# A decoder layer on one core: eight small parameter loads asked for behind the 25th load of raw tiles

## The chip, the core and the metric

The kernel runs on one core of a Trainium2 chip. A core has five engines that run side by side and meet at semaphores: TensorE (PE in the profile, with its weight loads as PEld), VectorE (DVE), ScalarE (ACT), GpSimd (POOL) and SyncE (SP). Here SP does no arithmetic: it issues every transfer, one after the other, and sixteen DMA engines carry them out. The metric is device microseconds of one execution. Three runs of the kernel before took 2458.3, 2456.9 and 2456.46 us, a median of 2456.9 us.

## The reference

One layer of a decoder trunk, batch 1, 2048 rows of 1024 values, all in float32:

```
proj = x @ w_in                     # 1024 -> q, k, v (8 heads x 64), b, c, h (256 each), p (256)
attn = stick_breaking_attention(q, k, v)         # sigmoid gates, products over the later keys, causal
conv = b * causal_conv3(c * h, conv_w)
pool = (window means of p over 2, 4, 8, 16, minus p) @ pool_w * pool_scale
mix  = rms_norm per 64 columns of [attn, conv, pool], times mix_norm_g
x1   = layer_norm(2**0.25 * x + mix @ w_o) * ln1_g + ln1_b
out  = layer_norm(2**0.25 * x1 + relu(x1 @ w_up)**2 @ w_down) * ln2_g + ln2_b
```

The small parameters of the change are `conv_w`, `pool_w` (four 64x64 blocks), `pool_scale`, `mix_norm_g` and `rcount`, a table of one over the number of rows in a window for the first 16 rows.

## The kernel before

Every large product is made of three: each float32 operand is split into a high part (rounded to the matmul's format by ACT) and a low part (the rest, by DVE or POOL), and PE adds high x high, high x low and low x high. `load` does this for the operands of the projections: SP issues the DMA of a raw tile of 128x512 values (L180), ACT casts it (L182), DVE or POOL subtracts (L184). The raw tiles, of x and of the weights alike, go through a ring of `RAW = 4` buffers, so the load of a tile waits on SP until the tile four loads back has been subtracted.

The 2048 rows are four chunks of 512. `qkv(cs)` projects two chunks: for a head group first k (`proj_qk` with `kscr`), then q, then v (`proj_v`). A projection of one chunk and 256 columns is two PSUM banks (`dn`, two buffers) of 24 matmuls each. A bank is emptied by `split`: a cast on ACT (L65, for q with a scale L68) and a subtraction on DVE (L66, L69) into `qk`, which SP writes to DRAM in four pieces per bank (L271, L272). Attention reads k, q and v back from there (L425, L409, L410, L427) and goes through units of 128 queries by 512 keys: a score matmul (`z`, L433), two sigmoids on ACT, a scan on DVE (L443, L446), a product on POOL (L448), transposes (`tp`, L465) and the product with v (`o`, L470, L471). After attention's chunks come `bchp` (conv and pool projections), the output projection and the first norm (`out_stage`), then the up and the down product.

The order of the work is not the order of the code. A scheduler places the instructions of all stages into one queue per engine before the kernel is built, by its own estimate of when each can start and by priorities: `early()` is the highest (loads, casts, subtractions, emptying of banks), attention is next, the projections are last, so PE fills attention's pauses with projections. Each engine then takes its queue strictly in order: an instruction that must wait holds up all that stand behind it. A change anywhere may give the scheduler other estimates, and other queues, for all that follows.

The eight loads of the change stand in the code ahead of everything that uses x: `gain` (L149), `cw` (L151), `psc` (L153), `rcount` (L155) and two pieces each of `pw0` and `pw1` (L160, L161). `gain` is read when a mixer's output is normalised (L302), `cw` in `conv` (L332 to L334), `rcount` and `pw` in the pool mixer (L358, L370), `psc` behind it (L372).

Of the kernel before, what the change touches and what calls it, by code (L numbers as in the profile page):

```python
# [17 lines left out]
P = 128  # L18
# [6 lines left out]
HD = 64  # L25
# [18 lines left out]
def build(nc, tc, ctx, A, out):  # L44
# [78 lines left out]
    with ExitStack() as up:  # L123
        pools = phase1(nc, tc, ctx, up, A, ident, scr, hscr, split, rsqrt, layer_norm, bcast)
# [3 lines left out]
def phase1(nc, tc, whole, ctx, A, ident, scr, hscr, split, rsqrt, layer_norm, bcast):  # L128
# [17 lines left out]
    nc.gpsimd.affine_select(last[:, CH + OFF - P - 1:], last[:, CH + OFF - P - 1:], pattern=[[-1, P + 1]],  # L146
                            compare_op=ALU.not_equal, fill=1.0, base=0, channel_multiplier=1)
    gain = p.tile([P, ND], F, name="gain")
    nc.sync.dma_start(gain, A["mix_g"])  # L149
    cw = pd.tile([P, 2, 3], F, name="cw")  # L150
    nc.sync.dma_start(cw, A["conv_w"])  # L151
    psc = pd.tile([P, 2], F, name="psc")
    nc.sync.dma_start(psc, A["pool_scale"])  # L153
    rcount = pd.tile([P, 2, 16], F, name="rcount")
    nc.sync.dma_start(rcount, A["rcount"])  # L155
    pw = []
    for i in range(2):
        w = pd.tile([P, P], F, name=f"pw{i}")
        nc.vector.memset(w, 0.0)
        nc.sync.dma_start(w[0:HD, 0:HD], A["pool_w"][2 * i])  # L160
        nc.sync.dma_start(w[HD:P, HD:P], A["pool_w"][2 * i + 1])  # L161
        pw.append(w)
    ucar = pd.tile([P, 2, 2], F, name="ucar")
    nc.vector.memset(ucar, 0.0)
# [3 lines left out]
    def early():  # L168
        return tc.high_priority(2 * PRIO)

    count = [0]

    def low_engine():
        count[0] += 1
        return nc.vector if (count[0] % 3 == 0) == (count[0] >= START) else nc.gpsimd

    def load(src, name, shape, bufs):
        pool = px if name == "x" else pm
        raw = pd.tile(shape, F, name=f"{name}raw", tag="raw", bufs=RAW)
        nc.sync.dma_start(raw, src)  # L180
        h = pool.tile(shape, R, name=f"{name}h", tag=f"{name}h", bufs=bufs)
        nc.scalar.copy(h, raw)  # L182
        l = pool.tile(shape, R, name=f"{name}l", tag=f"{name}l", bufs=bufs)
        low_engine().tensor_tensor(l, raw, h.bitcast(F), ALU.subtract)  # L184
        return h, l

    def load_w(g, x=None):

        w, xt = [], []
        with early():  # L190
            for q in range(4):
                w.append(load(A["w_in"][g][q], "w", [P, 2, 256], ND))
                if x is not None:
                    xt += [load_x(x, d) for d in (2 * q, 2 * q + 1)]
        return w, xt

    def load_x(c, d):
        return load(A["xt"][c][d], "x", [P, CH], 2 * ND)
# [42 lines left out]
    def proj_v(xs, g):  # L241
        for c, w, x in operands(xs, 4 + g):
            for jj in range(2):
                ps = dense_ps().rearrange("p (j e) -> p j e", j=2)
                for j in range(2):
                    ts = slice((2 * jj + j) * P, (2 * jj + j + 1) * P)
                    for d in range(ND):
                        wh, wl = (t[:, d % 2, :] for t in w[d // 2])
                        xh, xl = (t[:, ts] for t in x[d])
                        nc.tensor.matmul(ps[:, j, :], xh, wh, start=(d == 0), stop=False)  # L250
                        nc.tensor.matmul(ps[:, j, :], xh, wl, start=False, stop=False)
                        nc.tensor.matmul(ps[:, j, :], xl, wh, start=False, stop=(d == ND - 1))
                with early():
                    vst = pd.tile([P, 2, 4, P], R, name="vst", tag="big", bufs=3)
                    pv = ps.rearrange("p j (h x) -> p j h x", h=4)
                    split(vst[:, :, :, 0:HD], vst[:, :, :, HD:P], pv)
                    for j in range(2):
                        nc.sync.dma_start(vscr[c][g][:, :, 2 * jj + j, :].rearrange("h p x -> p h x"),
                                          vst.bitcast(F)[:, j])
                tick()  # L260

    def proj_qk(xs, g, scr, scale):
        for c, e, ps in proj_t(xs, g):
            with early():
                hl = pd.tile([P, 2, CH], R, name="qk", tag="big", bufs=3)
                hi, lo = hl[:, 0], hl[:, 1]
                split(hi, lo, ps, scale)
                for hh in range(2):
                    t = scr[c][4 * (g % 2) + 2 * e + hh]
                    rows = slice(hh * HD, (hh + 1) * HD)  # L270
                    nc.sync.dma_start(t[0], hi.bitcast(F)[rows])  # L271
                    nc.sync.dma_start(t[1], lo.bitcast(F)[rows])  # L272

    def qkv(cs):
        xs = [(c, []) for c in cs]
        for g in range(2):
            proj_qk(xs, 2 + g, kscr, None)
            proj_qk(xs, g, qscr, 0.125)
            proj_v(xs, g)
# [104 lines left out]
    def attention(c, pairs):  # L384
        for i in pairs:
            mix = {}
            for hh in range(2):
                head(c, 2 * i + hh, mix)

    def run(end=False):  # L390

        while units:
            units.pop(0)()
            turn[0] += 1
            if turn[0] > 5:
                blocks.pop(0)()
        while end and blocks:
            blocks.pop(0)()
            turn[0] = 0
        while end and soon:  # L400
            soon.pop(0)[1]()
# [89 lines left out]
    def load_wo(part):  # L491
        with early():
            w = [[load(A["w_o"][e][:, dd * CH:(dd + 1) * CH], "x", [P, CH], 2 * ND) for e in part] for dd in range(2)]
        wo.extend(zip(*w))
# [75 lines left out]

    turn_out = Turn(nc, tc, pd, ident, tscr, bank, {"b0": "pb", "b1": "pc", "c0": "pa", "x1h": "cs", "x1l": "cs"}, 4, early)

    for cs in ((0, 1), (2, 3)):
        qkv(cs)
        with tc.high_priority(PRIO):
            for pairs in ((0, 1), (2, 3)):
                for c in cs:
                    attention(c, pairs)
            run(True)
# [388 lines left out]
```

## Time and profile before

| | us |
|---|---|
| median of three runs | 2456.9 |
| the profiled execution | 2459.65 |
| its span (first to last instruction) | 2457.9 |
| PE busy in it | 2398.0 |
| DVE busy | 1589.8 |
| POOL busy | 1136.3 |
| ACT busy | 1008.2 |

The span is that of the engines' instructions; the profiled execution's own time is 1.75 us longer. "Busy" of PE is the time in which a matmul is under way; matmuls overlap, so two that stand side by side in a list start closer together than their durations say. A row of the timeline gives a start, a busy time, engine, line, operation and tiles, how many instructions are merged in it, and in brackets the idle time ahead of it with the instruction that ended it.

### The profile page before, as it was taken

To read this page: it belongs to the slowest core of one execution; us is meant where nothing else is said; L and a number is where in the kernel's file an instruction comes from. 1 tells how busy PE (TensorE), PEld (TensorE's weight loads), DVE (VectorE), ACT (ScalarE), POOL (GpSimd) and SP (SyncE) were. 2 spreads that over 40 slices of the span, in tenths; PEclk is the share of its full clock that TensorE was granted. 3 is DMA by queue.
4 is the path that set the end of the run, shared out by engine and by line. 5 is a ranking of instruction groups with operands and counts; after the bars stand their busy time and mean duration, and the time that the engine had idled before them with its cause. 6 is when DMAs were issued, how large, how long until landed. Compare 5 with 4: busy or idle time off the path is not lost.

```text
span 2457.9 us, 33072 instructions
## 1 busy us (share of the span) xinstructions
PE 2398.0 (98%) x11728; PEld 1992.8 (81%) x11728; DVE 1589.8 (65%) x2227; ACT 1008.2 (41%) x1945; POOL 1136.3 (46%) x833
## 2 busy tenths in 40 slices
PE   8999999999999999999999999999999999999997
PEld 6988888778778787788888888888888888888886
DVE  3778777788987899976666656556316433333367
ACT  4667666655666656522333223222332101111123
POOL 2557555864775757634556545555201101101137
PEclk9999999999999999999999999999999999999999
DMA  8758645622422446557665383333525312212212
GB/s 239 193 148 235 174 138 148 195 78 91 158 82 95 141 149 220 201 216 289 221 225 192 112 333 125 116 103 112 173 75 172 110 53 86 86 49 78 80 60 112
DMA packets 164854, 360.37 MB, mean 147 GB/s; under 512 B 18640, under 2 KB 35024, under 8 KB 162896
## 3 DMA queue, kind: packets, MB, share of 16 engines
q1 hardware_dynamic: 164688, 358.25, 45.2%
q8 instruction: 93, 1.52, 0.3%
q14 instruction: 73, 0.60, 0.1%
HBM read 245.19 MB, written 112.98 MB: 146 GB/s over the span
## 4 chain that ended last, share of the span: by engine, by line
PE 78%; DVE 9%; DMA 4%; POOL 4%; issue 3%; ACT 2%; SPq 1%; DVEq 0%; ACTq 0%; POOLq 0%
PE dn L895 9%; PE dn L894 9%; PE dn L893 9%; PE b L792 7%; PE c L792 4%; PE a L792 4%; PE z L433 4%; PE dn L235 3%; PE dn L236 3%; PE b L795 3%; PE dn L237 3%; PE tp L465 3%; PE c L795 2%; PE a L795 2%; PE dn L521 2%
## 5 line engine op out<-in xcount | busy, mean ns | idle before, releaser
L448 POOL TENSOR_TENSOR g<-g,sig 128x512 f32<-128x512 f32 (+2 forms) x320 | 381.6, 1197 | 338.3 <-DVE g L446 144.4
L893 PE MATMUL dn<-d,ht 128*128 128x512 f32 x1024 | 398.3, 389 | 0.0
L894 PE MATMUL dn<-d,ht 128*128 128x512 f32 x1024 | 398.3, 389 | 0.0
L895 PE MATMUL dn<-d,ht 128*128 128x512 f32 x1024 | 397.7, 389 | 0.0
L732 POOL TENSOR_TENSOR w<-raw,w 128x512 fp32r<-128x512 f32 x186 | 253.9, 1371 | 240.9 <-ACT w L731 240.9
L899 DVE TENSOR_TENSOR y<-dn,y 128x512 f32<-128x512 f32 x224 | 154.2, 689 | 322.2 <-PE dn L895 322.1
L858 POOL TENSOR_TENSOR d<-draw,d 128x1024 fp32r<-128x1024 f32 x32 | 77.6, 2438 | 507.4 <-ACT d L857 507.2
L446 DVE TENSOR_TENSOR_SCAN g<-beta,g,z 128x513 f32<-128x513 f32 x192 | 244.1, 1275 | 48.5 <-ACT sig L438 46.3
L436 ACT ACTIVATE beta<-z 128x512 f32<-128x512 f32 (+2 forms) x320 | 172.9, 541 | 159.4 <-PE z L433 146.3
L871 ACT CAST ht<-draw 128x512 fp32r<-128x512 f32 x128 | 74.5, 620 | 380.3 <-PE dn L895 347.3
L895 PEld LDWEIGHTS dn<-d,ht 128*128 128x128 f32 x1024 | 192.2, 188 | 39.9
L893 PEld LDWEIGHTS dn<-d,ht 128*128 128x128 f32 x1024 | 192.2, 188 | 39.9
L894 PEld LDWEIGHTS dn<-d,ht 128*128 128x128 f32 x1024 | 192.2, 188 | 39.9
L731 ACT CAST w<-raw 128x512 fp32r<-128x512 f32 x186 | 114.1, 621 | 252.9 <-PE b L795 143.8
L235 PE MATMUL dn<-xh,wh 128*128 128x512 f32 x512 | 206.9, 407 | 10.3 <-DVE qk L66 5.3
L433 PE MATMUL z<-k,q 128*128 128x512 f32 (+3 forms) x640 | 192.6, 380 | 17.8 <-DVE g L446 12.7
L236 PE MATMUL dn<-xl,wh 128*128 128x512 f32 x512 | 206.8, 404 | 0.0
L237 PE MATMUL dn<-xh,wl 128*128 128x512 f32 x512 | 206.7, 404 | 0.0
L469 DVE TENSOR_TENSOR tl<-tp,th 128x512 fp32r<-128x512 f32 (+1 forms) x320 | 184.3, 596 | 30.3 <-ACT th L468 29.5
L465 PE MATMUL tp<-ident,g 128*128 128x128 f32 x1088 | 190.8, 274 | 1.9 <-DVE tl L469 0.8
L792 PE MATMUL b<-x,w 128*128 128x512 f32 x768 | 190.2, 390 | 2.1 <-ACT w L731 1.5
L468 ACT CAST th<-tp 128x512 fp32r<-128x512 f32 (+1 forms) x320 | 161.5, 535 | 63.9 <-PE tp L465 51.9
(195 smaller groups left out, 4983.9 us busy)
## 6 DMA issues: line engine op xcount, KB each, us to landing
hscr<-h SPq DMA_DIRECT2D x128, 256.0 KB, 2.8
draw<-hscr SPq DMA_DIRECT2D x64, 512.0 KB, 3.9
raw<-in_w_up SPq DMA_DIRECT2D x62, 512.0 KB, 4.4
x<-tscr SPq DMA_DIRECT2D x14, 2048.0 KB, 12.3
wraw<-in_w_in SPq DMA_DIRECT2D x80, 256.0 KB, 3.3
k<-kscr SPq DMA_DIRECT2D x80, 256.0 KB, 3.0
v<-vscr SPq DMA_DIRECT2D x80, 256.0 KB, 2.8
xraw<-in_xt SPq DMA_DIRECT2D x64, 256.0 KB, 3.1
```

What stands on the lines that cost most here:

```text
L235: nc.tensor.matmul(ps, wh, xh, start=(d == 0), stop=False)
L236: nc.tensor.matmul(ps, wh, xl, start=False, stop=False)
L237: nc.tensor.matmul(ps, wl, xh, start=False, stop=(d == ND - 1))
L433: nc.tensor.matmul(z[:, 0:w], q[:, b, j * P:(j + 1) * P], m["k"][:, 0:w], start=(b == 0), stop=(b == 1))
L446: nc.vector.tensor_tensor_scan(left, rev, idle, st["prev"][j][:, OFF - 1:OFF], ALU.mult, ALU.bypass)
L448: nc.gpsimd.tensor_tensor(gv, gv, sig[:, 0:w], ALU.mult)
L465: nc.tensor.transpose(out=tp[:, j * P:(j + 1) * P], in_=m["g"][j][:, cols], identity=ident)
L732: self.nc.gpsimd.tensor_tensor(w[:, 1], src, w.bitcast(F)[:, 0], ALU.subtract)
L792: nc.tensor.matmul(ps, wk[:, 0, d], x[:, i, :, d, :], start=(first and d == 0 and i == 0), stop=False, skip_group_check=True)
L893: nc.tensor.matmul(ps, hh[:, ts], dh[:, ds], start=(i == 0), stop=False)
L894: nc.tensor.matmul(ps, hh[:, ts], dl[:, ds], start=False, stop=False)
L895: nc.tensor.matmul(ps, hl[:, ts], dh[:, ds], start=False, stop=(i == 3))
```

## The change

The eight loads leave the head of the program. A function `parameters` issues them once, after the first `qkv`, and holds each of them behind the 25th raw tile's load: twelve loads belong to the first chunk (four weight tiles, eight of x), eight to the second chunk's x, four to the weights of the second projection, and the 25th is the first weight tile of the third. The zeroing of `pw` by DVE stays where it was. What is loaded, and into which tiles, is the same.

```diff
     gain = p.tile([P, ND], F, name="gain")
-    nc.sync.dma_start(gain, A["mix_g"])
     cw = pd.tile([P, 2, 3], F, name="cw")
-    nc.sync.dma_start(cw, A["conv_w"])
     psc = pd.tile([P, 2], F, name="psc")
-    nc.sync.dma_start(psc, A["pool_scale"])
     rcount = pd.tile([P, 2, 16], F, name="rcount")
-    nc.sync.dma_start(rcount, A["rcount"])
     pw = []
     for i in range(2):
         w = pd.tile([P, P], F, name=f"pw{i}")
         nc.vector.memset(w, 0.0)
-        nc.sync.dma_start(w[0:HD, 0:HD], A["pool_w"][2 * i])
-        nc.sync.dma_start(w[HD:P, HD:P], A["pool_w"][2 * i + 1])
         pw.append(w)
...
-    count = [0]
+    count, loads = [0], []
...
-        nc.sync.dma_start(raw, src)
+        loads.append(nc.sync.dma_start(raw, src))
...
+    def parameters():
+        ld = [(gain, A["mix_g"]), (cw, A["conv_w"]), (psc, A["pool_scale"]), (rcount, A["rcount"])]
+        for i in range(2):
+            ld += [(pw[i][0:HD, 0:HD], A["pool_w"][2 * i]), (pw[i][HD:P, HD:P], A["pool_w"][2 * i + 1])]
+        with tc.issue_after(loads[24].ins):
+            for dst, src in ld:
+                nc.sync.dma_start(dst, src)
+
     for cs in ((0, 1), (2, 3)):
         qkv(cs)
+        if not cs[0]:
+            parameters()
```

In the changed kernel most lines stand six lines higher: L174, L176 and L178 are `load`'s three lines, L265 and L266 the writes of `qk`, L440 and L463 attention's scan and its subtraction; L573 is the new issue.

SP's queue at the start of the program, before (from the fourth load on; `wraw` and `xraw` are raw tiles of weights and of x):

```order
L180 DMA wraw<-in_w_in 128x512
L149 DMA gain<-in_mix_g 128x8
L151 DMA cw<-in_conv_w 128x6
L153 DMA psc<-in_pool_scale 128x2
L180 DMA xraw<-in_xt 128x512
L155 DMA rcount<-in_rcount 128x32
L180 DMA xraw<-in_xt 128x512
L160 DMA pw_271<-in_pool_w 64x64
L180 DMA wraw<-in_w_in 128x512
```

SP's queue of the changed kernel where the first of the eight now stands, behind the eight writes of the first chunk's `qk`:

```order
L174 DMA xraw<-in_xt 128x512
L174 DMA wraw<-in_w_in 128x512 x3
L419 DMA k<-kscr_0_100 128x512
L419 DMA k<-kscr_1_101 128x512
L174 DMA wraw<-in_w_in 128x512 x4
L573 DMA gain<-in_mix_g 128x8
L265 DMA kscr_0_108<-qk 64x512
L266 DMA kscr_0_108<-qk 64x512
```

The first twelve raw loads now follow each other with nothing between; the other seven of the eight stand further down, among the writes of the next `qk` tiles. Ahead of attention's reads of `k` there were two loads of `xraw` and two of `wraw`; now there are one and three, and the other `xraw` stands ahead of the eight writes.

ACT's queue around the emptying of the first two pairs of PSUM banks, before (`xh` and `wh` are casts of raw tiles, `qk` the emptying; numbers count tiles upwards):

```order
L182 CAST xh_437<-xraw_435 128x512
L65 CAST qk_384<-dn_359 128x512
L65 CAST qk_416<-dn_391 128x512
L182 CAST xh_443<-xraw_441 128x512
L182 CAST xh_449<-xraw_447 128x512
L182 CAST xh_455<-xraw_453 128x512
L182 CAST xh_461<-xraw_459 128x512
L182 CAST xh_467<-xraw_465 128x512
L182 CAST wh_537<-wraw_535 128x512
L182 CAST wh_543<-wraw_541 128x512
L65 CAST qk_496<-dn_471 128x512
L65 CAST qk_528<-dn_503 128x512
```

The same place of the changed kernel, where the tiles of the first part have numbers that are lower by 8:

```order
L176 CAST xh_435<-xraw_433 128x512
L65 CAST qk_376<-dn_351 128x512
L65 CAST qk_408<-dn_383 128x512
L176 CAST xh_441<-xraw_439 128x512
L176 CAST xh_447<-xraw_445 128x512
L176 CAST xh_453<-xraw_451 128x512
L176 CAST xh_459<-xraw_457 128x512
L176 CAST wh_529<-wraw_527 128x512
L176 CAST wh_535<-wraw_533 128x512
L176 CAST wh_541<-wraw_539 128x512
L65 CAST qk_488<-dn_463 128x512
L65 CAST qk_520<-dn_495 128x512
```

Tile `xh_443` of before is `xh_435` here: its cast has moved from behind the first emptying to ahead of it. One more weight tile's cast (`wh_541`, before `wh_549`) has moved ahead of the second. DVE's queue has the subtractions of the same two tiles moved in the same way.

DVE's queue where the pool mixer of the first chunk meets attention, before (`g` are attention's scans, `pl` the pool mixer's window means, `mixr` a finished head):

```order
L446 SCALAR_TENSOR_TENSOR g<-beta_283,g,z 128x513
L469 TENSOR_TENSOR tl<-tp,th 128x384
L184 TENSOR_TENSOR wl<-wraw,wh 128x512
L340 COPY pcar<-pa 128x15
L485 TENSOR_TENSOR mixr<-o,mixr 64x512
L469 TENSOR_TENSOR tl<-tp,th 128x256
L358 TENSOR_TENSOR pl<-pb,rcount 64x16
L360 SCALAR_TENSOR_TENSOR pl<-pb,pa 64x496
L359 TENSOR_TENSOR pl<-pl,pa 64x16
L446 SCALAR_TENSOR_TENSOR g<-beta_285,g,z 128x513
L446 SCALAR_TENSOR_TENSOR g<-beta_283,g,z 128x513
```

The same place of the changed kernel:

```order
L440 SCALAR_TENSOR_TENSOR g<-beta_277,g,z 128x513
L463 TENSOR_TENSOR tl<-tp,th 128x512
L463 TENSOR_TENSOR tl<-tp,th 128x384
L178 TENSOR_TENSOR wl<-wraw,wh 128x512
L334 COPY pcar<-pa 128x15
L352 TENSOR_TENSOR pl<-pb,rcount 64x16
L354 SCALAR_TENSOR_TENSOR pl<-pb,pa 64x496
L353 TENSOR_TENSOR pl<-pl,pa 64x16
L440 SCALAR_TENSOR_TENSOR g<-beta_275,g,z 128x513
L479 TENSOR_TENSOR mixr<-o,mixr 64x512
L463 TENSOR_TENSOR tl<-tp,th 128x256
L440 SCALAR_TENSOR_TENSOR g<-beta_277,g,z 128x513
```

The finished head and one of attention's subtractions have moved from ahead of the next scan to behind it; another subtraction (128x512) stands in their place. Moves of this size are found on every engine all through attention, and the queue of PE is the same again only from about its 5,500th of some 11,600 instructions on.

## Rows read from the trace of the kernel before

**Rows 1.** The page's first line.

```profile
span 2457.9 us, 33072 instructions
```

**Rows 2.** Busy time by stage: stretch, length, then each engine, granted clock, DMA share.

```profile
0.00:36.00 36.00, 25.99 (x99) 19.94 (x100) 14.54 (x30) 17.53 (x29) 10.50 (x17) 1.00 0.77 226
36.00:200.00 164.00, 164.00 (x1021) 146.10 (x1020) 118.03 (x161) 100.82 (x222) 81.56 (x71) 1.00 0.68 187
...
450.00:1050.00 600.00, 569.41 (x2938) 459.90 (x2937) 526.99 (x741) 370.99 (x746) 395.57 (x306) 0.99 0.43 138
```

**Rows 3.** Timeline of SP's queue, 2 to 12 us.

```profile
5.09 0.43 SPq L155 DMA_DIRECT2D rcount<-in_rcount  x1
5.62 0.38 SPq L180 DMA_DIRECT2D xraw<-in_xt  x1
...
10.48 0.59 SPq L161 DMA_DIRECT2D pw<-in_pool_w  x1
11.17 0.53 SPq L180 DMA_DIRECT2D wraw<-in_w_in  x1
```

**Rows 4.** DMA issues at 17.50, 30.26, 7.87 and 4.72 us; last: us to landing.

```profile
xraw<-in_xt SPq DMA_DIRECT2D x1, 256.0 KB, 3.9
...
wraw<-in_w_in SPq DMA_DIRECT2D x1, 256.0 KB, 5.0
...
wraw<-in_w_in SPq DMA_DIRECT2D x1, 256.0 KB, 2.6
...
xraw<-in_xt SPq DMA_DIRECT2D x1, 256.0 KB, 3.2
```

**Rows 5.** Timeline around PE's first pause, 19 to 23 us.

```profile
19.18 1.30 ACT L182 CAST xh<-xraw 128x512 fp32r<-128x512 f32 x2 [1.38 <-DMA xraw<-in_xt]
20.38 1.07 ACT L65 CAST qk<-dn 128x512 fp32r<-128x512 f32 x2
20.99 1.29 DVE L66 TENSOR_TENSOR qk<-dn,qk 128x512 fp32r<-128x512 f32 x2 [0.47 <-ACT qk L65]
21.45 1.24 ACT L182 CAST xh<-xraw 128x512 fp32r<-128x512 f32 x2
21.74 0.50 PE L235 MATMUL dn<-xh,wh 128*128 128x512 f32 x1 [2.95 <-DVE qk L66]
...
22.20 1.28 DVE L184 TENSOR_TENSOR xl<-xraw,xh 128x512 fp32r<-128x512 f32 x2
```

**Rows 6.** Timeline around PE's second pause, 26 to 36 us.

```profile
26.05 1.03 SPq L180 DMA_DIRECT2D xraw<-in_xt  x2
...
27.17 0.86 SPq L180 DMA_DIRECT2D wraw<-in_w_in  x2
...
30.26 4.79 SPq L180 DMA_DIRECT2D wraw<-in_w_in  x4
...
32.18 1.29 ACT L182 CAST wh<-wraw 128x512 fp32r<-128x512 f32 x2 [1.86 <-DMA wraw<-in_w_in]
...
33.37 1.07 ACT L65 CAST qk<-dn 128x512 fp32r<-128x512 f32 x2
...
34.61 1.28 DVE L66 TENSOR_TENSOR qk<-dn,qk 128x512 fp32r<-128x512 f32 x2
...
35.34 0.50 PE L235 MATMUL dn<-xh,wh 128*128 128x512 f32 x1 [2.38 <-DVE qk L66]
```

**Rows 7.** Instructions on tile gain: ns min/median/max, first to last start.

```profile
L302 DVE SCALAR_TENSOR_TENSOR oa<-mixr,gain,msp x16: 693/733/750, 116.2 to 1065.4; 128x512 f32<-128x512 f32 x16
```

**Rows 8.** Short windows of PE: length, busy, granted clock, DMA share.

```profile
20.00:22.00 2.00, 0.26 (x1) 1.00 0.57 175
...
480.00:485.00 5.00, 4.01 (x13) 0.62 0.20 57
485.00:490.00 5.00, 5.00 (x18) 0.69 0.00 0
```

**Rows 9.** Timeline of PE, 475 to 484 us.

```profile
479.32 0.73 PE L433 MATMUL z<-k,q 128*128 128x512 f32 x2 [2.84 <-DVE g L446]
```

## Prediction

> **What bounds the kernel now.** I read the stages first. The span is 2457.9 us [rows 1], and PE is what fills it: from 36 to 200 us it is busy for all of the 164.00 us, and from 450 to 1050 us it is busy 569.41 of 600 us while DVE is busy 526.99 [rows 2]. So a microsecond that PE loses in the first 36 us is not given back by anything up to 200 us: whatever is late at 36 us stays late. The first stretch holds 10.01 us of idle PE (36.00 - 25.99) [rows 2]; the timeline shows where: until the first tile is there, then a pause of 2.95 us that ends at 21.74 [rows 5] and one of 2.38 us that ends at 35.34 [rows 6]. Both pauses end with DVE's subtraction L66: PE has filled both PSUM banks of a block and can start the next only when ACT has cast a bank and DVE has subtracted it. The change touches exactly this stretch, so I looked at what stands ahead of those casts.
>
> **The change part by part.**
>
> *What goes.* Eight issues on SP, 0.43 to 0.59 us each [rows 3], together some 4 us. Most of them lie in time in which SP waits for a free raw buffer anyway. Two are seen to hold a tile up: `rcount`, issued from 5.09 to 5.52, ahead of the tile at 5.62, and the last piece of `pw`, 10.48 to 11.07, ahead of the weight tile at 11.17 [rows 3]. The chain that ends the first block runs through other tiles, so their lateness costs nothing by itself. What the chain can gain is a less crowded set of DMA engines. Bounds: nothing, or what one tile could land faster; the tile issued at 4.72, just behind three parameters, took 3.2 us and the fastest 2.6 [rows 4], so the upper end is 0.6 us. I take 0.3 us, an estimate in the middle.
>
> *What moves on ACT and DVE, first pause.* Before, ACT does five casts of the second chunk's and the first block's last tiles and then empties the banks at 20.38; the cast of the next tile, `xh_443`, comes behind it, at 21.45 [rows 5]. In the changed queue that cast stands ahead of the emptying, and DVE's subtraction of the same tile ahead of L66. The tile was issued at 17.50 and took 3.9 us, so it landed at 21.4 [rows 4]: an empty place has become a wait for a DMA. With the gain of 0.3 us it lands at 21.1. Then one cast of 0.62 (half of 1.24) to 21.72, one emptying cast of 0.53 (half of 1.07) to 22.25; DVE subtracts the tile from 21.75 to 22.4 (half of 1.28) and the bank to 23.05 (half of 1.29); PE starts 0.1 us behind that, as it did before, at 23.15 instead of 21.74 [rows 5]: 1.4 us late. Lower end: the tile lands in 2.6 us [rows 4] from 17.2; the casts of the two tiles ahead of it end at 20.48 - 0.3 [rows 5], and the same steps from there give 22.2, 0.5 us late. Upper end: no gain at the start, 21.4 and 23.45, 1.7 us late.
>
> *Second pause.* The block between the pauses ran from 21.74 to 32.96 (35.34 - 2.38), 11.2 us without a stop [rows 5, 6]; started at 23.15 it ends at 34.35. Before, two weight tiles were cast from 32.18 on and the emptying followed at 33.37; the third weight tile was issued at 30.26 [rows 6] and took 5.0 us [rows 4], after the emptying had begun. In the changed queue its cast, and its subtraction on DVE, stand ahead of the emptying. But its load comes sooner too: it needs the buffer of the tile `xraw_459`, which was held behind the eight writes of `qk` until 26.05 [rows 6] and now goes ahead of them. The writes start 1.3 us later than before, with the first emptying; one tile of x less stands behind them (half of 1.03), so the three weight tiles are issued at about 28.0, 28.4 and 28.9 (before, 27.17 and 0.43 later for the first two). By 5.0 us each the third lands at 33.9; the first lands at 33.0 and three casts of 0.65 take ACT to 34.9, the emptying cast to 35.45; DVE subtracts the third tile by 35.6 (0.65) and the bank by 36.25; PE starts at 36.35 instead of 35.34: 1.0 us late in all, since this pause has become a little shorter. Lower end: weight tiles that land in 2.6 us, so that nothing stands in the way; the block started 0.5 us late (22.2) ends at 33.45, and the emptying alone (0.53, 0.65 and 0.1) would start PE at 34.75, earlier than before by 0.6. Upper end: 23.45 + 11.2 + 2.38 = 37.05, 1.7 us late. I take +1.0 us, since the tiles' landing times in just this stretch are those that I used, and keep -0.6 to +1.7.
>
> *What is added at 35 to 60 us.* The eight issues again, some 4 us of SP's time, among the writes of k and q and attention's first reads; each pushes back all that stands behind it on SP. PE has the projections of q and v in its queue and was never idle from 36 to 200 us [rows 2], so I cost it at nothing; without that cover it would be up to 8 x 0.5 = 4 us. The readers are far: `gain` is first read at 116.2 us [rows 7], the other parameters later.
>
> *The queues behind.* No work is added, but attention's queues are shuffled on all engines until about 1030 us. In 450 to 1050 us PE idles 30.59 us [rows 2], in pieces of at most 2.84 us [rows 9]; a shuffle trades some of them for others. I see no direction in that and take 0, with some 5 us to each side: two of the longest pieces, or one together with the clock (below).
>
> Sum: +1.0 us. The profiled execution took 2459.65 us, 2.75 us above the median; with the change it would be 2460.7, and against the median 2456.9 + 1.0 = 2457.9 us. A measurement of this kernel tells a change from none at about 0.2%, 4.9 us here, that is below 2452.0 or above 2461.8. The forecast is no change that can be told.
>
> **The clock.** [...] Behind the pause of 2.95 us at 21.74 it stayed at 1.00 [rows 8]. [...]
>
> **The rivals.**
> - *The clock falls in the lengthened pauses.* For it: the fall at 480 us behind a shorter pause. Against it: the two pauses of before, which did not cool it. One fall gives 2457.9 + 3.45 = 2461.4, still no change that can be told; a fall in each of the two pauses gives 2464.8, slower. It decides if the granted clock is below 0.9 behind both.
> - *Attention's stop at 479 us goes.* Before, a finished head and a subtraction stand on DVE ahead of the scan that PE waits for; in the changed queue they stand behind it. For it: the scan L446 ends the longest pause of the trace [rows 9]. Against it: the pool mixer's window means still stand ahead of that scan. If the pause and the fall of the clock both went: -2.84 - 3.45 + 1.0 = -5.3, 2451.6 us, faster.
> - *The shuffle goes the other way*: one more such stop, 2.84 + 3.45 us, gives 2464.2, slower.
> - *The cover at 35 to 60 us isn't enough*: SP's 4 us reach PE, 2461.9, at the edge of slower. Against it: 164 us without a pause of PE.
> - *The start gains and the pauses don't grow*: the lower ends, -0.6, 2456.3, no change.
>
> **How the numbers follow.** Forecast 0.52, its own range 2453 to 2462. Clock 0.14, of which both pauses 0.08. The stop at 479 us goes 0.18. The shuffle goes the other way 0.09. SP's cover 0.05, of which 0.03 above the edge. No longer pauses 0.02. Faster: 0.18. Slower: 0.08 + 0.09 + 0.03 = 0.20. The rest, 0.62, within 0.2%. The range reaches to the centres of the cases on either side and a little beyond: 2450 to 2466 us.
>
> **What would show it.** In the changed trace: ACT's cast of the fourth tile of the second chunk ahead of the first emptying and waiting for its DMA; a pause of PE above 4 us that ends at about 23 us and one of about 2 us that ends near 36 us; the clock at 1.00 behind both; no idle PE from 37 to 200 us, although SP issues the eight loads there. It is wrong if the first pause is not longer than 2.95 us, if PE pauses while SP issues the parameters, or if the idle time of PE between 450 and 1050 us differs from 30.6 us by more than 5 us.

## The result, and the profile after

The changed kernel takes 2470.93 us, the median of four runs (2470.21 to 2473.95); the kernel before took 2457.6 beside it (2456.46 to 2458.3). The ratio is 1.0059, with a 95% interval of 1.0046 to 1.0072: slower by 0.59%, some 14 us. The forecast was 2457.9 and no change, its range 2450 to 2466. The profiled execution took 2470.92 us; its page begins so (before, [rows 1]):

```profile
span 2469.1 us, 33064 instructions
```

The span is 11.2 us longer (the profiled execution of the kernel before, 2459.65 us, was its slowest, so the medians lie a little further apart). The table by stage has the columns of [rows 2]: the stretch, its length, busy time of PE, PEld, DVE, ACT and POOL, the granted clock, the DMA share.

```profile
0.00:36.00 36.00, 27.37 (x96) 20.34 (x96) 13.84 (x28) 16.88 (x28) 10.79 (x17) 0.95 0.77 228
36.00:200.00 164.00, 162.63 (x1009) 145.09 (x1010) 112.40 (x156) 97.79 (x215) 81.07 (x70) 1.00 0.68 187
450.00:1050.00 600.00, 565.88 (x2916) 457.88 (x2916) 516.22 (x731) 369.69 (x748) 395.91 (x306) 0.98 0.43 136
```

Against [rows 2], PE is busy longer in the first 36 us with fewer matmuls (96 for 99): the clock is 0.95 for 1.00, and a matmul's mean busy time 0.285 us (27.37 / 96) for 0.263. Of the 1.37 us idle in the second stretch 0.79 are the second pause, which now ends at 36.79. In the third PE is idle 3.53 us more (569.41 - 565.88), and the clock is 0.98 for 0.99.

A landmark, a matmul that stands at the same place of both queues, shows that the whole loss lies ahead of the up product. PE's matmuls are the same in both kernels from the 5,632nd of 11,728 on; that one starts at 1065.08 us before and at 1076.26 after. One matmul of the up product, in the timeline of PE before (start, busy time, engine, line, operation, count, idle time ahead with what ended it):

```profile
1141.41 1.43 PE L792 MATMUL b<-x,w 128*128 128x512 f32 x5 [1.50 <-ACT w L731]
```

The same matmul after:

```profile
1152.90 1.43 PE L796 MATMUL b<-x,w 128*128 128x512 f32 x5 [1.57 <-ACT w L735]
```

It comes 11.5 us later, and the spans differ by 11.2. Up to there the loss divides into idle PE and a lower clock. Before and after, the first 1200 us of each trace:

```profile
0.00:1200.00 1200.00, 1153.27 (x6218) 963.28 (x6219) 949.96 (x1350) 690.44 (x1409) 707.49 (x568) 0.99 0.55 169
```

```profile
0.00:1200.00 1200.00, 1147.93 (x6164) 957.89 (x6165) 938.91 (x1341) 683.96 (x1402) 700.52 (x562) 0.99 0.55 168
```

PE idles 5.3 us more. The clock is rounded too far here; added up over windows of 10 us (each window's length times one minus its clock) it took 8.5 us before and 11.9 after. That is 8.7 of the 11.2 us. The rest is in neither sum; matmuls that wait a little while they count as busy would not show there, but that this is the rest is not shown.

The idle time is spread out. Between 40 and 1080 us PE pauses 54 times before, 33.8 us in all, and 68 times after, 39.3 us. All but one of the pauses before, and all but two of those after, are shorter than 2.2 us.

The first pause, after (timeline; answers to [rows 5]):

```profile
21.04 0.62 ACT L176 CAST xh<-xraw 128x512 fp32r<-128x512 f32 x1 [0.81 <-DMA xraw<-in_xt]
21.56 1.06 ACT L65 CAST qk<-dn 128x512 fp32r<-128x512 f32 x2
21.68 0.69 DVE L178 TENSOR_TENSOR xl<-xraw,xh 128x512 fp32r<-128x512 f32 x1 [2.08 <-ACT xh L176]
...
22.29 1.28 DVE L66 TENSOR_TENSOR qk<-dn,qk 128x512 fp32r<-128x512 f32 x2
...
23.03 0.50 PE L229 MATMUL dn<-xh,wh 128*128 128x512 f32 x1 [3.76 <-DVE qk L66]
```

ACT's cast waits for its tile's DMA until 21.04, the emptying stands behind it, and PE's pause is 3.76 us instead of 2.95. The clock behind it, after and then before:

```profile
23.00:30.00 7.00, 6.97 (x23) 5.61 (x24) 2.23 (x3) 1.28 (x3) 1.57 (x1) 0.76 0.88 234
```

```profile
23.00:30.00 7.00, 7.00 (x32) 5.82 (x31) 0.95 (x2) 1.54 (x3) 1.29 (x1) 1.00 0.94 240
```

The second pause, after (answers to [rows 6]):

```profile
33.06 0.62 ACT L176 CAST wh<-wraw 128x512 fp32r<-128x512 f32 x1 [0.33 <-DMA wraw<-in_w_in]
...
35.43 1.07 ACT L65 CAST qk<-dn 128x512 fp32r<-128x512 f32 x2 [1.75 <-PE dn L231]
...
36.05 1.29 DVE L66 TENSOR_TENSOR qk<-dn,qk 128x512 fp32r<-128x512 f32 x2 [1.64 <-ACT qk L65]
...
36.79 0.50 PE L229 MATMUL dn<-xh,wh 128*128 128x512 f32 x1 [0.95 <-DVE qk L66]
```

Here the weight tiles were cast in good time: ACT waits 1.75 us for PE, not for a DMA. PE is late (36.79, before 35.34) because the block between the pauses ran at the lower clock (0.76 from 23 to 30 us).

The pause of [rows 9] did not go: 2.81 us, ended by the same scan. And behind the start the longest pause that before doesn't have ends at 958.57:

```profile
482.19 0.74 PE L427 MATMUL z<-k,q 128*128 128x512 f32 x2 [2.81 <-DVE g L440]
...
955.65 0.62 ACT L176 CAST wh<-wraw 128x512 fp32r<-128x512 f32 x1 [2.45 <-DMA wraw<-mscr]
...
956.30 1.61 DVE L178 TENSOR_TENSOR wl<-wraw,wh 128x512 fp32r<-128x512 f32 x1 [1.34 <-ACT wh L176]
...
957.13 1.08 ACT L462 CAST th<-tp 128x512 fp32r<-128x512 f32 x2
...
957.84 0.68 DVE L548 SCALAR_TENSOR_TENSOR r<-r,dn 128x512 f32<-128x512 f32 x1
...
958.57 0.64 PE L654 MATMUL dn<-ident,r 128*128 128x128 f32 x3 [2.81 <-DVE r L548]
```

It has the shape of the first pause, some 930 us later: ACT's cast of a raw tile waits for its DMA, DVE's subtraction of that tile waits for the cast, and the norm's sum, for which PE waits, stands behind it in DVE's in-order queue.

### The profile page after: what moved, and what is told of

It reads as the page before. It is cut to its first block, busy times and chain, and to the rows that moved or that the text cites. A ratio compares the mean times of both kernels' runs of the same rounds, so it can differ in the third digit from the quotient of the medians.

```text
span 2469.1 us, 33064 instructions
## 1 busy us (share of the span) xinstructions
PE 2403.8 (97%) x11728; PEld 1998.1 (81%) x11728; DVE 1589.6 (64%) x2227; ACT 1005.6 (41%) x1945; POOL 1137.1 (46%) x833
## 4 chain that ended last, share of the span: by engine, by line
PE 79%; DVE 9%; DMA 4%; POOL 3%; issue 2%; ACT 2%; SPq 0%; DVEq 0%; ACTq 0%; POOLq 0%
PE dn L899 9%; PE dn L898 9%; PE dn L897 9%; PE b L796 7%; PE c L796 4%; PE a L796 4%; PE z L427 4%; PE dn L229 4%; PE dn L231 4%; PE dn L230 3%; PE b L799 3%; PE tp L459 3%; PE c L799 2%; PE a L799 2%; DVE g L440 2%
## 5 line engine op out<-in xcount | busy, mean ns | idle before, releaser
L440 DVE TENSOR_TENSOR_SCAN g<-beta,g,z 128x513 f32<-128x513 f32 x192 | 244.1, 1276 | 54.1 <-ACT sig L432 53.1
L463 DVE TENSOR_TENSOR tl<-tp,th 128x512 fp32r<-128x512 f32 (+1 forms) x320 | 184.3, 597 | 23.1 <-ACT th L462 22.2
## 6 DMA issues: line engine op xcount, KB each, us to landing
x<-tscr SPq DMA_DIRECT2D x14, 2048.0 KB, 12.8
```

The costliest lines, as they stand in the source:

```text
L440: nc.vector.tensor_tensor_scan(left, rev, idle, st["prev"][j][:, OFF - 1:OFF], ALU.mult, ALU.bypass)
```

## The experiments

Theory Q: the loss is the shuffled queues of attention. Rivals: L, the late loads cost it themselves (SP's time, or parameters that come too late); S, the lengthened pauses at the start. To part them I needed kernels with the loads in one place and the queues of the other. Such a kernel builds the program, takes the order that the scheduler gave each engine, builds it again, and ties each instruction to the one ahead of it on its engine; the eight loads stay free:

```diff
+def program(bacc, shapes, late, wanted=None):
...
+                if i.engine in behind:
+                    tc.add_manual_dep(i, behind[i.engine], mybir.DependencyInfo(
+                        mybir.DependencyClass.NoSync, mybir.DependencyReason.DATA), reason="order")
+                behind[i.engine] = i.name
...
+def final(bacc, shapes):
+    old = program(bacc, shapes, False)[1]
+    return program(bacc, shapes, True, old)[0]
```

This is e1 (loads late, queues of before). In e2 to s9 and f1 only `final` differs; n1 and n2 leave the scheduler free.

**e1.** 

> The eight loads are issued late, as in the change, but every engine's other instructions are held in exactly the order of the kernel before. Theory Q (the shuffled queues cost the time, the loads' place costs nothing): 2457 us, within 2 us of the kernel before, perhaps 0.5 us faster. Theory L (late issues among the writes of q and k cost it): 2468 to 2471 us. Theory S (the longer pauses at the start cost it): 2457 us, as the emptying casts stand where they stood.

**e2.** The loads at the head, the changed kernel's queues:

```diff
-    old = program(bacc, shapes, False)[1]
-    return program(bacc, shapes, True, old)[0]
+    new = program(bacc, shapes, True)[1]
+    return program(bacc, shapes, False, new)[0]
```

> The eight loads are issued at the head, as before, but every engine's other instructions are held in exactly the order of the changed kernel. Theory Q: 2470 us, within 2 us of the changed kernel. Theory L: 2457 to 2459 us. Theory S: 2470 us, since both pauses stay.

**e3, e4.** Two orders joined at the 300th of 17,704 instructions (about 50 us), the loads late; e4 has `False` and `True` the other way round:

```diff
+    order = {late: program(bacc, shapes, late)[1] for late in (False, True)}
+    return program(bacc, shapes, True, spliced(order[True], order[False], [300]))[0]
```

> Late loads; the first 300 instructions of the joined order (about the first 50 us) stand in the changed kernel's order, all others in that of the kernel before. Theory S: 2468 to 2471 us if the start is all of it. Theory Q, with the loss spread over attention: 2457 + 1.5 (the lateness of PE at 36 us) = about 2459 us.

> Late loads; the first 300 instructions stand in the order of the kernel before, all others in the changed kernel's. Theory S: 2457 to 2459 us. Theory Q, with the loss spread over attention: 2470.9 - 1.5 = about 2469 us.

| | loads | queues of the changed kernel | ratio to before | 95% interval |
|---|---|---|---|---|
| e1 | late | none | 1.0004 | 0.9995 to 1.0012 |
| e2 | at the head | all | 1.0066 | 1.0053 to 1.0078 |
| e3 | late | to 50 us | 1.0008 | 0.9999 to 1.0017 |
| e4 | late | from 50 us on | 1.0053 | 1.0041 to 1.0066 |

L falls: with the old queues the late loads cost nothing that can be told. Q is shown: the new queues cost all of it with the loads at their old place. The traces bear out that the orders are the ones meant: e1 has the matmuls and the instructions of ACT and DVE one for one in the order of the kernel before, e2 in that of the changed kernel. S is at most a small part: the new start alone, with its longer pause, is +0.08%, 2 us, at the edge of what can be told (behind the second pause PE restarts at 36.06 us in e3's trace and at 34.30 in e1's).

**n1, n2.** Is it this place alone, or any move? The hold behind another tile, the scheduler free:

```diff
-        with tc.issue_after(loads[24].ins):
+        with tc.issue_after(loads[12].ins):
```

(n2: `loads[20]`.) 

> The eight loads are held behind the 13th raw load instead of the 25th, and the scheduler is left free. Its queues then differ from those of the kernel before at 14 places of PE's and 2 each of ACT's and DVE's, not at thousands. Theory Q (the queues cost it): 2456 to 2458 us. A theory by which any later place of the loads costs time: 2460 us or more.

> The eight loads are held behind the 21st raw load, scheduler free. Its queues are a third set: PE's differs at some 4,400 places from either kernel's. Theory R (a shuffle has no direction): any time from 2450 to 2475 us, most likely not the same as the changed kernel's 2470.9. Theory D (a late place of the loads has a cost of its own through the scheduler's estimates): 2468 to 2473 us, as the changed kernel.

n1 is 1.0000 (0.9990 to 1.0010), n2 1.0095 (1.0077 to 1.0113). In n1 the scheduler's queues differ from those of before at 14 places of PE and two each of ACT and DVE; in n2, by the traces, at some 4,600 of PE's 11,728 matmuls (the changed kernel's at some 4,700). The price follows the shuffle, not how late the loads are: the 21st tile costs more than the 25th.

**s5 to s9.** Which stretch of the new queues costs? All with the loads at the head; for s5:

```diff
+    return program(bacc, shapes, False, spliced(order[True], order[False], [4400]))[0]
```

> Early loads; the first 4,400 of 17,704 instructions of the joined order (to about 460 us) stand in the changed kernel's order, the rest in that of the kernel before. By the idle time of PE in the two traces the loss lies partly here: start and 200 to 250 us, together about 4 us: 2461 us. If the first half of attention is free: 2457 us; if it holds all of the loss: 2470 us.

> Early loads; the first 7,000 instructions (to about 775 us) stand in the order of the kernel before, the rest in the changed kernel's. By the idle time of PE in the two traces some 8 to 11 us of the loss lie behind 775 us: 2466 us. If the loss is made earlier: 2457 to 2459 us.

> The loads stay at the head. The queues are those of before up to the 4400th instruction of the joined order (about 460 us), those of the changed kernel to the 7000th (about 775 us), and then those of before again. Theory of sums (each stretch of the new queues has a price of its own, and these add up): the first stretch alone cost 7.8 us and the last alone 14.6, together 22.4, while the whole cost 15.0 (with early loads); so the middle must give back some 7 us: 2450 us, faster by 0.3%, and in the trace PE's idle time between 550 and 750 us is some 4 us less than before. Rival, no sums: what a stretch costs hangs on where the work stands that meets it, so the middle alone gives nothing: 2457 to 2459. Rival, seams: each change of order costs by itself: 2460 or more.

> The loads stay at the head. The changed kernel's queues only from the 7000th to the 8300th instruction of the joined order (about 775 to 925 us), those of before ahead of it and behind. The whole from 7000 on cost 14.6 us. Theory (the price is many small stops, in the stretches where DVE is 80 to 99% busy): about half of it here, 2463 to 2466, with no single pause of PE above 2.5 us in the stretch that before doesn't have. Rival (one bad place, the pause of 2.81 us that ends at 958 us in the changed kernel and the lower clock behind it): nothing here, 2457 to 2459, and all of it in the kernel that takes the new queues from 8300 on.

> The loads stay at the head. The changed kernel's queues only from the 8300th instruction of the joined order on (about 925 us; from about 1054 us on both are the same). Theory of many small stops: the other half of the 14.6 us, 2463 to 2466, with a pause of 2.8 us near 950 us as one part of it (2.8 + some 3 us of clock). Rival (one bad place): all of it, 2470 to 2473. Rival (the price comes from how the two stretches meet): 2457 to 2459 here and in the kernel with 7000 to 8300 alone, though both together cost 14.6.

| | new queues in | ratio | 95% interval | x 2457.8 us |
|---|---|---|---|---|
| s5 | 0 to 460 us | 1.0026 | 1.0015 to 1.0038 | +6.4 |
| s6 | 460 to 775 us | 0.9995 | 0.9987 to 1.0004 | -1.2 |
| s7 | 775 us on | 1.0063 | 1.0047 to 1.0079 | +15.5 |
| s8 | 775 to 925 us | 1.0044 | 1.0031 to 1.0057 | +10.8 |
| s9 | 925 us on | 1.0026 | 1.0017 to 1.0035 | +6.4 |

s8 and s9 together give 17.2 us, s7 15.5; s5, s6 and s7 give 20.7, e2 16.2: the stretches add up within their intervals. The middle gives nothing back, so s6, from which I had hoped for 2450, is no better kernel. The "one bad place" falls too: s8, which has the old queues from 925 us on, still pauses at 958 us, and s9, which has the new ones there, doesn't: its longest pause from 900 to 1030 us is 1.67. PE in s8, then in s9:

```profile
958.65 1.11 PE L657 MATMUL dn<-ident,r 128*128 128x128 f32 x4 [2.81 <-DVE x1l L635]
```

```profile
940.66 0.61 PE L525 MATMUL dn<-xh,wh 128*128 128x512 f32 x1 [1.67 <-DVE r L558]
```

So what stands ahead has a part in which tile is late when the same queue meets it, and part of a stretch's price is paid behind it. s8's dearest stretches against those of before show both halves of the price, idle PE and the clock. Before:

```profile
850.00:900.00 50.00, 46.78 (x247) 38.66 (x245) 45.18 (x68) 31.93 (x64) 32.91 (x26) 0.97 0.51 161
...
950.00:1000.00 50.00, 48.61 (x256) 39.37 (x255) 48.66 (x78) 29.09 (x60) 28.41 (x24) 1.00 0.56 189
```

s8:

```profile
850.00:900.00 50.00, 47.26 (x234) 38.52 (x234) 44.95 (x64) 29.49 (x60) 35.26 (x28) 0.92 0.48 151
...
950.00:1000.00 50.00, 46.13 (x231) 37.78 (x230) 43.93 (x68) 26.84 (x54) 29.73 (x23) 0.93 0.62 207
```

DVE is busy for 88 to 97% of these stretches in both kernels, which leaves it little idle time to make up a delay; that this is why the delays add up is argued, not shown.

**f1.** Are the casts that wait for a DMA the cause? The changed kernel, its own queues, three casts and their subtractions moved behind attention's:

```diff
+    order = program(bacc, shapes, True)[1]
+    for k, front in ((7702, 5139), (7705, 7702), (7703, 5133), (7706, 5134),
+                     (8286, 6048), (8287, 6028), (8691, 6525), (8692, 8643)):
+        order.remove(k)
+        order.insert(order.index(front) + 1, k)
+    return program(bacc, shapes, True, order)[0]
```

> The changed kernel with its own queues, the late loads included, but for three places of ACT's queue (at 658, 844 and 955 us of the changed kernel's trace). In each a cast of a raw tile waits for its DMA (2.81, 1.55 and 2.45 us) and attention's casts stand behind it; here the cast stands behind them, and so do the subtractions of the same tiles on DVE and POOL. PE's queue and SP's are unchanged. Theory (the loss of the new queues is made of casts that wait for a transfer ahead of work that PE waits for): PE's pauses of 2.19, 1.27 and 2.81 us at 662, 847 and 959 us go or shrink below 1 us, 6.3 us at most, and with them the lower clock behind them (up to 5 us): 2460 to 2466 instead of 2470.9. Rival (the tile is then late by as much, and PE or SP waits for it a few microseconds later): the pauses go but come back as others, 2469 to 2472. Rival (the pauses have another cause, since DVE and POOL are busy there for 90% of the time): they stay, 2470.9.

1.0048 (1.0034 to 1.0061): 1.1 parts in a thousand below the changed kernel, not told apart from it. The trace shows why the gain is small. At 958 us of the changed kernel, f1 has:

```profile
952.52 0.65 DVE L558 SCALAR_TENSOR_TENSOR r<-r,dn 128x512 f32<-128x512 f32 x1
...
953.91 1.65 DVE L188 TENSOR_TENSOR wl<-wraw,wh 128x512 fp32r<-128x512 f32 x1 [0.74 <-ACT wh L186]
...
955.49 0.68 DVE L635 TENSOR_TENSOR x1l<-dn,x1h 128x512 fp32r<-128x512 f32 x1
...
956.31 0.47 PE L525 MATMUL dn<-xh,wh 128*128 128x512 f32 x1 [2.20 <-DVE x1l L635]
```

The sum that PE waited for now goes ahead of the late tile, but the next thing that PE needs, `x1l`, stands behind it: 2.81 became 2.20. At 662 us 2.19 became 0.81 and a new pause of 1.49; at 847 us 1.27 became 0.72. Since both have the same PE queue, the time won can be read from PE's landmarks either side of each place (the matmuls that the changed kernel starts at 650 and 700, 840 and 900, 945 and 970 us): 0.5, 1.0 and 0.6 us, 2.1 of the 6.3. So the mechanism is real at these places and taking it away pays about a third; that it makes up the whole loss is not shown. The profiled executions differ by 5.2 us, but chance is in that: 1.6 us of it comes at about 540 us, ahead of the first edit, where the granted clock was 0.83 in the changed kernel (535 to 545 us) and 1.00 in f1.

Over all fourteen profiled kernels the sum of idle PE and clock to 1200 us (windows of 10 us, as above) follows the span to within some 7 us: s6 53.7, e3 55.0, before 55.2, n1 55.4, s5 57.6, s9 58.7, e1 59.8, f1 62.0, e4 63.6, after 64.0, s7 64.4, s8 65.3, e2 69.7, n2 77.8 us. The span less this sum lies between 2398.0 and 2405.3 in every one, while the spans run from 2454.6 to 2479.0. A few microseconds it can't tell: e1's sum is 4.6 above that of before, and their spans are 2457.8 and 2457.9.

One thing was not tried: every new queue here is that of all engines at once, so which engine's order carries the price stays open.

## Why the prediction was wrong

- *What goes, +0.3.* Not borne out, and the time of the cast (21.04, forecast 21.1) came out by luck. The tile was issued at 18.04 us, where the kernel before issued it at 17.50, and took 3.0 us instead of the 3.9 that I used; the first block ended at 19.27 (23.03 - 3.76), 0.5 us later than before, where I had it 0.3 earlier. The other runs can't tell a gain: with the old queues PE restarted at 20.58 and 21.02 with late loads (e1, e4) and at 20.93 to 21.74 with early ones (before, s6 to s9).
- *First pause.* Right in its mechanism, a cast that waits for its DMA ahead of the emptying, and in PE's start, 23.03 for 23.15. The pause is 3.76 us and not above 4, since the block ahead of it ended later.
- *Second pause.* Forecast 36.35, measured 36.79, but for another reason. The third weight tile, which I had landing too late (at 33.9; its cast began at 33.06), did not hold the emptying up, and the pause shrank to 0.95 us. What made PE late was the block ahead of it: 12.8 us (36.79 - 0.95 - 23.03) instead of 11.2, by the lower clock. The clock rival had this: it fell behind the first pause, to 0.76 from 23 to 30 us, which I estimate at 1.7 us (7 x 0.24), and not behind the second (1.00 from 37 to 44 us). The 3.45 us that the rivals take for one fall is 5 x 0.38 + 5 x 0.31, from the 0.62 and 0.69 that [rows 8] show over ten microseconds at 480 us; in the changed kernel no fall of that size stands behind either pause of the start.
- *The eight issues at 35 to 60 us, nothing.* Right: e1.
- *"The queues behind. ... I see no direction in that and take 0, with some 5 us to each side."* This is the step that failed. I put the term at 0 because I saw no direction; for this one shuffle it was some 12 us of loss (e4: 0.53% = 13; e2: 16; the start is 2). I bounded it by two of the longest pauses; but the shuffle reaches a thousand microseconds, and made many small stops there, most of them under 2.2 us, some with a lower clock behind them (0.62 from 665 to 670 us, behind the pause of 2.19 us at 662; 0.77 from 960 to 965 us, behind the 2.81 us that end at 958.57). My sign for it was too narrow as well: PE's idle time from 450 to 1050 us is 34.12 us for 30.59, within the 5 us that I allowed, while the loss is spread from the start to 1065 us and is in part clock. The rival "the shuffle goes the other way" had the sign, at 2464.2 and a chance of 0.09, with one stop where there were many.
- *The stop at 479 us goes.* It did not (2.81 us). The clock behind it stayed at 1.00 in the changed kernel (480 to 490 us), where before had 0.62 and 0.69 [rows 8].

I found no way to read the sign of the shuffle, or its size, from the trace of before. The runs give a width afterwards: n1, n2 and the changed kernel show 0, +0.95 and +0.59% for three places of the same eight loads, so a bound of 5 us was too narrow for queues that differ at thousands of places. Two such shuffles, both slower, say nothing of the sign of a third.

## What to carry to other kernels

In this kernel, whose in-order queues a scheduler sets, the price of moving eight small loads was that of the new queues (e2: 1.0066), not of the loads (e1: 1.0004): compare the queues first, and if they differ far behind the edit, widen the range by what such shuffles cost here (0.59 and 0.95%). To learn what the edit itself does, hold the old order and move only the loads; and place a hold where the queues stay (behind the 13th tile: 1.0000). In the new queues look for a cast or a subtraction that waits for a DMA ahead of work that TensorE needs; at three such places moving it won a third of the pauses (2.1 of 6.3 us).

## What the runs showed of the hardware

Whether a pause of 2 to 3 us costs clock could not be told from its length. Before, 2.84 us at 479 us were followed by 0.62 and 0.69 and 2.95 us at the start by 1.00 [rows 8]; after, 2.81 us at 482 us by 1.00 and 3.76 us at the start by 0.76. At the first pause the runs can be put side by side. In six kernels the late tile's cast stands ahead of both emptying casts (after, e2, e3, f1, n2, s5): the pause was 3.60 to 3.82 us, and the granted clock from 23 to 30 us was 0.62 to 0.78 in all six. That is a mean over 7 us: after, windows of 1 us read 0.50 from 24 to 27 us and 1.00 from 28 us on, and PE's matmuls start 0.43 us apart from 24.41 to 26.55 us and 0.23 us apart from 28.18 to 28.87. In the other eight it stands behind both (in n1 between them): 1.92 to 2.95 us, followed by 0.77 to 0.92 in five (e1, n1, s6, s7, s8) and by 1.00 in three (before, e4, s9). One of the five is s6, whose queues and loads are those of before up to 460 us; its first pause was shorter in its profiled execution, and the clock behind it lower. Its PE timeline, then the stretch behind the pause:

```profile
21.60 0.50 PE L239 MATMUL dn<-xh,wh 128*128 128x512 f32 x1 [2.18 <-DVE qk L66]
...
35.34 0.50 PE L239 MATMUL dn<-xh,wh 128*128 128x512 f32 x1 [0.95 <-DVE qk L66]
```

```profile
23.00:30.00 7.00, 7.00 (x26) 5.64 (x25) 0.97 (x2) 1.79 (x3) 1.28 (x1) 0.77 0.95 236
```

There the fall cost little, since the second pause shrank (0.95 us for 2.38): PE restarted at 35.34 as in [rows 6], 13.74 us behind the first restart, where the three runs without the fall took 13.60 (before), 13.07 (e4) and 12.76 (s9). So the clock was lower behind all six first pauses of 3.60 to 3.82 us, and behind five of the eight of 1.92 to 2.95 us; what decides in those is not shown. As an estimate from these readings, the price of one of the shorter pauses is a range: 0 (before, 1.00 behind 21.74 us) to 3.45 us (before, 0.62 and 0.69 behind 479.32).
